# First MLP layer with 512-column and 256-column matmuls per row tile, and a rearranged end chain

## The chip, the cores and the metric

The kernel runs on one core of a Trainium2 chip. The metric is the device time of one execution in microseconds (us); lower is better. The engines are named as in the profile: PE is TensorE's matmul, PEld its weight load, DVE is VectorE, ACT is ScalarE, POOL is GpSimd, and SP is SyncE, whose queue issues most DMAs.

## The reference

One layer of a decoder block over 256 tokens with 2048 channels, all in f32. A normalised input goes through one wide projection, three token mixers (attention, short convolution, a state-space scan) are merged and projected with `w_o`, and then come the parts that matter here:

```python
x = x + (merged @ w_o[i])
h = rms_norm(x, g_mlp[i])
x = x + (jnp.square(jax.nn.relu(h @ w_up[i])) @ w_down[i])     # 2048 -> 8192 -> 2048
gate = jax.nn.sigmoid(rms_norm(x, g_ple[i]) @ w_ple_gate[i])
x = x + ((p[i] @ w_ple[i]) * gate)
return rms_norm(x, g_final)
```

## The kernel before

**Arithmetic.** A product of f32 matrices is made of three matmuls. Each operand is split into a high part (ScalarE rounds it to the fp32r format, `split`, L163 or L166) and a low part (VectorE subtracts the high part from the source, L164 or L167). `mm3` (L171 to L173) issues high*high, high*low and low*high into one PSUM region.

**Weights.** All weights are read once, in pieces of 128 x 1024 f32 (512 KB: two row tiles of 128 by 512 columns), by SP's queue (L75) into six `raw` buffers. `Stream.convert` makes the high part on ScalarE (L87) and the low part on VectorE (L88) into one of four `w` buffers; both are emitted with `high_priority(offset=2000)`. `get(i)` converts one piece ahead of the one that it hands out. A `w` buffer comes free when the matmuls of its piece are done.

**Units.** `unit` computes 512 output columns over a contraction of 2048: four chunks `c`, in each two pieces, in each two row tiles `k`. Kind "A" keeps the tokens stationary and moves 512 weight columns (two token halves `m`, so six matmuls of 512 columns per row tile). Kind "B" keeps four 128-column blocks `s` of the weights stationary and moves the 256 tokens (twelve matmuls of 256 columns per row tile); its output comes out transposed, as the next product wants it. Where "B" is used in the MLP, high and low part of the tokens are two tiles of tag `aT`, eight buffers in all, and the four blocks lie in two PSUM banks.

**PSUM.** There are eight banks: four of tag `acc` for the units, four of tag `s` for transposes and small products.

**The MLP** runs in four quarters `q` of the hidden layer. A quarter has four up units (kind "B", `h2` moving), each followed by `act_job`: ReLU from PSUM on ScalarE (L1130), square on VectorE (L1131), split (L163, L164). Then come four down units (kind "A", `act` stationary), each followed by two VectorE instructions that add the two banks to `x1` (L1150).

**The end.** After the MLP come the gate units, four of kind "A". In the last one the matmuls of token half `m` = 0 come before those of `m` = 1, so that the chain of the first half starts earlier: sigmoid (L1191), multiplication by `pp` in place (L1195), sum with `x1` (L1196), sum of squares (L1198), reciprocal root (`rsqrt`, or L1206 to L1211 with ScalarE's Sqrt for the last one), scaling of four blocks of 512 columns (L1215 to L1221), and the output DMAs on SP's queue (L1223). `dummy` (L1193) is a two-element Sqrt that brings the activation table in early.

**Order.** The Tile framework puts the instructions of each engine in one fixed order, by priority (program order, moved forward by `high_priority`), by its own estimate of when operands are ready, and by when a buffer of the tag is free; each engine then runs its list in that order and waits on semaphores.

Of the kernel before, what the change touches and what calls it, by code (L numbers as in the profile page):

```python
# [15 lines left out]
D = 2048  # L16
T = 256
# [114 lines left out]
def _kern(tc, xT, xn, pT, pos, wbig, consts, colp, rowp, w2p, normg, gfin, cw, out):  # L132
# [24 lines left out]

    def ps(shape=(128, 512)):
        return psum.tile(list(shape), F32, tag="s", name="s", bufs=4)
# [98 lines left out]
    def aT(name):  # L258
        return sb.tile([128, 4, T], R32, tag="aT", name=name, bufs=8)

    hT = []
    for c in range(4):
        h, lo = aT("hTh"), aT("hTl")
# [4 lines left out]
        hT.append((h, lo))  # L268
# [140 lines left out]
    def renorm():  # L409
        for c in range(4):  # L410
            h, lo = aT("hNh"), aT("hNl")
            split(h, lo, xr[c])
            hN.append((h, lo))
# [508 lines left out]
    def unit(kind, lhs, accs, before=None, after=None, apart=False):  # L922

        for c in range(4):
            if before is not None:
                before(c)
            ah, al = lhs[c]
            if apart and c == 3:

                w = [(2, 1, last3)] + [(3, hf, piece()) for hf in range(2)]  # L930
                for m in range(2):
                    for cc, hf, (wh, wl) in w:
                        xh, xl = lhs[cc]
                        for k in range(2):
                            kk = 2 * hf + k
                            mm3(accs[m], (xh[:, kk, sl(m)], xl[:, kk, sl(m)]), (wh[:, k], wl[:, k]),
                                False, cc == 3 and kk == 3)
                break
            for hf in range(2):
                wh, wl = piece()  # L940
                if apart and c == 2 and hf == 1:
                    last3 = (wh, wl)
                    break
                for k in range(2):
                    kk = 2 * hf + k
                    first, last = c == 0 and kk == 0, c == 3 and kk == 3
                    if kind == "A":
                        for m in range(2):
                            mm3(accs[m], (ah[:, kk, sl(m)], al[:, kk, sl(m)]), (wh[:, k], wl[:, k]), first, last)
# [22 lines left out]
    for name, j, _ in units:  # L972
        if name == "small":
            a = acc((128, T))
            n = 0
            for q in range(2):
                wh, wl = piece()
                for k in range(8):
                    xh, xl = hN[n // 4]
                    mm3(a, (wh[:, k], wl[:, k]), (xh[:, n % 4], xl[:, n % 4]), n == 0, n == 15)  # L980
                    n += 1
                side.run(BUDGET)
# [94 lines left out]
    def before_wo(c):  # L1077
        if c == 3:
            side.finish()
        h, lo = aT("mTh"), aT("mTl")  # L1080
        split(h, lo, mg[c])
        mTs[c] = (h, lo)

    def norm_T(n, gains, dst, parts):

        h, lo = aT("h2h"), aT("h2l")
# [6 lines left out]
        dst[n] = (h, lo)  # L1093
# [28 lines left out]
    for q in range(4):  # L1122
        act = {}

        def act_job(a, n, accs):
            h, lo = b4([128, 4, T], R32, name="acth"), b4([128, 4, T], R32, name="actl")
            for i in range(2):
                t = tt([128, 512], name="a")
                with tc.high_priority(offset=1000):
                    S.activation(t, accs[i].rearrange("p s t -> p (s t)"), AF.Relu)  # L1130
                V.tensor_tensor(t, t, t, OP.mult)  # L1131
                split(h[:, sl(i, 2)], lo[:, sl(i, 2)], t.rearrange("p (s t) -> p s t", s=2))
            a[n] = (h, lo)

        for n in range(4):
            accs = [acc((128, 2, 256)) for _ in range(2)]
            if q == 0 and n == 0:
                unit("B", _Drain(h2, side), accs)
# [3 lines left out]
            else:  # L1142
                unit("B", h2, accs)
# [31 lines left out]
    xg, rs4 = {}, {}  # L1175
    for n in range(4):
# [6 lines left out]
        for m in range(2):  # L1183
            final = n == 3 and m == 1
            s4, r = (sm([128, 1], name=q) for q in ("s4", "r4")) if n == 3 else (None, None)
            prio = tc.high_priority(offset=2000) if final else ExitStack()
            with prio:
                parts = [slice(0, 256), slice(256, 512)] if final else [slice(0, 512)]
                s = tt([128, 512], name="sg")
                for q in parts:  # L1190
                    S.activation(s[:, q], accs[m][:, q], AF.Sigmoid, scale=rs3[:, m:m + 1])  # L1191
                if final:
                    S.activation(dummy, s[:, 510:512], AF.Sqrt)  # L1193
                for i, q in enumerate(parts):
                    V.tensor_tensor(s[:, q], s[:, q], pp[n][:, m, q], OP.mult)  # L1195
                    V.tensor_tensor(x1[n][:, m, q], x1[n][:, m, q], s[:, q], OP.add)  # L1196
                    sq = tt([128, 512], name="scr")
                    S.activation(sq[:, q], x1[n][:, m, q], AF.Square, accum_out=ss4[:, m, n + i:n + i + 1])  # L1198
                if not final:
                    G.tensor_tensor(pp[n][:, m], x1[n][:, m], gf[n], OP.mult)  # L1200
                if n < 3:
                    continue
                V.tensor_reduce(s4, ss4[:, m, 0:4 + m], axis=AX.X, op=OP.add)
                if final:
                    v, y, a = sm([128, 1], name="v"), sm([128, 1], name="y"), sm([128, 1], name="a")
                    V.tensor_scalar(v, s4, 1.0 / D, EPS, op0=OP.mult, op1=OP.add)  # L1206
                    S.activation(y, v, AF.Sqrt)
                    V.reciprocal(y, y)
                    V.scalar_tensor_tensor(a, y, -0.5, y, op0=OP.mult, op1=OP.mult)
                    V.tensor_tensor(a, a, v, OP.mult)  # L1210
                    V.scalar_tensor_tensor(r, a, 1.5, y, op0=OP.add, op1=OP.mult)  # L1211
                else:
                    rsqrt(r, s4, 1, D)
            if final:
                V.scalar_tensor_tensor(pp[3][:, m], x1[3][:, m], r, gf[3], op0=OP.mult, op1=OP.mult)  # L1215
                V.tensor_scalar(pp[1][:, m], pp[1][:, m], r, None, op0=OP.mult)
            else:
                for i in (1, 3):
                    G.tensor_tensor(pp[i][:, m], pp[i][:, m], bc(r, [128, 512]), OP.mult)
            S.activation(pp[0][:, m], pp[0][:, m], AF.Copy, scale=r)  # L1220
            S.activation(pp[2][:, m], pp[2][:, m], AF.Copy, scale=r)  # L1221
            for i in (0, 3, 1, 2):
                nc.sync.dma_start(out[:, m, sl(i, 512)], pp[i][:, m])  # L1223
# [98 lines left out]
```

## Time and profile before

| | |
|---|---|
| median of 3 runs | 2020.86 us (2019.52 to 2022.93) |
| the profiled execution | 2019.0 us, span 2017.0 us |
| granted TensorE clock, mean | 0.997 |
| busy share: PE, PEld | 99%, 87% |
| busy share: DVE, ACT, POOL | 66%, 51%, 3% |

Matmuls are pipelined and their recorded durations overlap, so the distance between the starts of two matmuls, and not their duration, is the time that one takes from the engine. Lines are those of the kernel before.

### The profile page before, as it was taken

The numbers are of one execution on the slowest core, as the hardware profiler recorded it, in microseconds if no ns is written. First come the engines' busy times: TensorE is split into PE (matmuls) and PEld (weight loads), VectorE is DVE, ScalarE is ACT, GpSimd is POOL, SyncE is SP. The second block draws the span as 40 slices with busy tenths as digits, with TensorE's granted clock in tenths as the row PEclk, the third lists the DMA queues.
The fourth block names the chain that finished last, engine by engine and source line by source line (L and its number), as shares of the span: only waits on it lengthen the run. The fifth ranks groups of instructions, "written<-read, shape, count | busy, mean of one in ns | idle before, by whom it ended". The sixth has DMA issues, their size and how long they took to land.

```text
span 2017.0 us, 29062 instructions
## 1 busy us (share of the span) xinstructions
PE 1995.5 (99%) x11221; PEld 1747.1 (87%) x11221; DVE 1325.3 (66%) x2095; ACT 1024.3 (51%) x1369; POOL 69.5 (3%) x93
## 2 busy tenths in 40 slices
PE   9999999999999999999999999999999999999997
PEld 7899988898888888898888899889988998998886
DVE  8877768766777668776878665555555555555665
ACT  7556646454655455544645464434433443445554
POOL 1000000000000000000000000000000000000011
PEclk9999999999999999999999999999999999999998
DMA  8556666555665565656675555555555555565552
GB/s 336 188 186 211 194 204 203 194 195 176 211 204 199 174 203 202 206 171 199 208 248 179 184 178 180 190 196 183 183 194 191 180 188 196 186 201 189 187 188 104
DMA packets 110267, 392.91 MB, mean 195 GB/s; under 512 B 12628, under 2 KB 13012, under 8 KB 110128
## 3 DMA queue, kind: packets, MB, share of 16 engines
q1 hardware_dynamic: 103552, 368.71, 54.8%
q0 software_dynamic: 6576, 22.34, 3.6%
q8 instruction: 88, 1.44, 0.3%
q14 instruction: 51, 0.42, 0.1%
HBM read 386.75 MB, written 4.25 MB: 194 GB/s over the span
## 4 chain that ended last, share of the span: by engine, by line
PE 51%; DVE 1%; issue 0%; ACT 0%; DMA 0%; POOLq 0%; POOL 0%; ACTq 0%
PE acc L171 17%; PE acc L173 17%; PE acc L172 17%; PE s L431 1%; DVE w L88 0%; DMA cv<-scrx 0%; PE s L171 0%; PE s L173 0%; PE s L172 0%; PE s L850 0%; ACT L720 0%; ACT scr L1198 0%; POOLq L1315 0%; DVE x L1196 0%; ACT w L87 0%
## 5 line engine op out<-in xcount | busy, mean ns | idle before, releaser
L88 DVE TENSOR_TENSOR w<-raw,w 128x1024 fp32r<-128x1024 f32 x686 | 840.0, 1225 | 587.9 <-ACT w L87 585.7
L87 ACT ACTIVATE w<-raw 128x1024 fp32r<-128x1024 f32 x686 | 726.1, 1059 | 827.8 <-PE acc L173 698.4
L171 PE MATMUL acc<-w,hNh 128*128 128x512 f32 x1024 | 403.9, 394 | 0.0
L173 PE MATMUL acc<-w,hNl 128*128 128x512 f32 x1024 | 399.3, 390 | 0.0
L172 PE MATMUL acc<-w,hNh 128*128 128x512 f32 x1024 | 399.2, 390 | 0.0
L171 PE MATMUL acc<-h2h,w 128*128 128x256 f32 x1024 | 290.0, 283 | 0.0
L173 PE MATMUL acc<-h2h,w 128*128 128x256 f32 x1024 | 289.8, 283 | 0.0
L172 PE MATMUL acc<-h2l,w 128*128 128x256 f32 x1024 | 289.8, 283 | 0.0
L173 PEld LDWEIGHTS acc<-w,hNl 128*128 128x128 f32 x1024 | 192.2, 188 | 41.2
L172 PEld LDWEIGHTS acc<-w,hNh 128*128 128x128 f32 x1024 | 192.5, 188 | 37.2
L171 PEld LDWEIGHTS acc<-w,hNh 128*128 128x128 f32 x1024 | 192.3, 188 | 37.2
L171 PE MATMUL acc<-w,acth 128*128 128x512 f32 x512 | 199.8, 390 | 0.0
L173 PE MATMUL acc<-w,actl 128*128 128x512 f32 x512 | 199.3, 389 | 0.0
L172 PE MATMUL acc<-w,acth 128*128 128x512 f32 x512 | 199.2, 389 | 0.0
L172 PEld LDWEIGHTS acc<-h2l,w 128*128 128x128 f32 x1024 | 196.6, 192 | 0.1
L171 PEld LDWEIGHTS acc<-h2h,w 128*128 128x128 f32 x1024 | 196.6, 192 | 0.1
L173 PEld LDWEIGHTS acc<-h2h,w 128*128 128x128 f32 x1024 | 196.6, 192 | 0.0
L171 PE MATMUL acc<-hNh,w 128*128 128x256 f32 x464 | 132.4, 285 | 0.0
L173 PE MATMUL acc<-hNh,w 128*128 128x256 f32 x464 | 131.3, 283 | 0.0
L172 PE MATMUL acc<-hNl,w 128*128 128x256 f32 x464 | 131.2, 283 | 0.0
L173 PEld LDWEIGHTS acc<-w,actl 128*128 128x128 f32 x512 | 96.1, 188 | 20.1
L172 PEld LDWEIGHTS acc<-w,acth 128*128 128x128 f32 x512 | 96.2, 188 | 19.6
(358 smaller groups left out, 2428.0 us busy)
## 6 DMA issues: line engine op xcount, KB each, us to landing
raw<-wbig SPq DMA_DIRECT2D x686, 512.0 KB, 3.3
cv<-scrx POOLq DMA_DIRECT2D x16, 512.0 KB, 6.1
cw<-cw POOLq DMA_DIRECT2D x8, 512.0 KB, 5.5
E<-acsd POOLq DMA_DIRECT2D x16, 256.0 KB, 4.8
xb<-xn SPq DMA_DIRECT2D x4, 512.0 KB, 10.0
scrx<-ev POOLq DMA_DIRECT2D x4, 512.0 KB, 5.5
x<-xn SPq DMA_DIRECT2D x4, 512.0 KB, 7.1
out<-pp SPq DMA_DIRECT2D x8, 256.0 KB, 2.2
```

What stands on the lines that cost most here:

```text
L87: nc.scalar.activation(w[:, 0], s, AF.Copy)
L88: nc.vector.tensor_tensor(w[:, 1], s, w[:, 0].bitcast(F32), OP.subtract)
L171: PE.matmul(o, ah, bh, start=start, stop=False)
L172: PE.matmul(o, ah, bl, start=False, stop=False)
L173: PE.matmul(o, al, bh, start=False, stop=stop)
L431: PE.transpose(p[:, sl(g)], src[:, sl(g)], ident)
```

## The change

1. The `aT` tiles become [128, 4, 2, T] with high and low part of a row tile side by side (four buffers in place of eight halves); `part` picks one part where a kind "A" unit wants it.
2. A new kind "P" replaces "B" in the MLP's up units. Per row tile it issues four matmuls of 512 columns (weight high part against both parts of the tokens) and then four of 256 (weight low part against the tokens' high part). Each block `s` has a PSUM bank of its own, `[128, 2, T]`; a unit takes four banks, from tag `acc` for even `n` and from tag `s` for odd `n`.
3. `act_job` joins the two halves of each bank first: ScalarE copies the second half to SBUF, VectorE adds the first half to it (`join`). ReLU and square then are one VectorE instruction, max(t,0)*t.
4. In the end chain, the multiplication by `pp` writes a new tile `t`; the second part's sum of squares moves to VectorE; of the first half only block 0 is scaled ahead of the last chain, and its other three blocks wait for `r1`, a copy of `r0` that VectorE makes after the last chain's reciprocal; GpSimd scales nothing more; the seven output DMAs that are left are issued in a new order, one of them on ScalarE's queue.

```diff
+    def halves(tag):
+        return [psum.tile([128, 2, T], F32, tag=tag, name="half", bufs=4) for _ in range(4)]
...
     def aT(name):
-        return sb.tile([128, 4, T], R32, tag="aT", name=name, bufs=8)
+        return sb.tile([128, 4, 2, T], R32, tag="aT", name=name, bufs=4)
+
+    def part(a, i, kk, q):
+        return a[i][:, kk, q] if isinstance(a, tuple) else a[:, kk, i, q]
...
                     else:
                         for s in range(4):
-                            mm3(accs[s // 2][:, s % 2], (wh[:, k, sl(s)], wl[:, k, sl(s)]), (ah[:, kk], al[:, kk]),
-                                first and s % 2 == 0, last and s % 2 == 1)
+                            PE.matmul(accs[s], wh[:, k, sl(s)], a[:, kk], start=first, stop=False)
+                        for s in range(4):
+                            PE.matmul(accs[s][:, 0], wl[:, k, sl(s)], a[:, kk, 0], start=False, stop=last)
...
+    def join(dst, u, a):
+        S.activation(u, a[:, 1], AF.Copy)
+        V.tensor_tensor(dst, a[:, 0], u, OP.add)
...
             for i in range(2):
-                t = tt([128, 512], name="a")
+                t, u = tt([128, 2, T], name="a"), tt([128, 2, T], name="al")
                 with tc.high_priority(offset=1000):
-                    S.activation(t, accs[i].rearrange("p s t -> p (s t)"), AF.Relu)
-                V.tensor_tensor(t, t, t, OP.mult)
-                split(h[:, sl(i, 2)], lo[:, sl(i, 2)], t.rearrange("p (s t) -> p s t", s=2))
+                    for s in range(2):
+                        join(t[:, s], u[:, s], accs[2 * i + s])
+                V.scalar_tensor_tensor(t, t, 0.0, t, op0=OP.max, op1=OP.mult)
+                split(h[:, sl(i, 2)], lo[:, sl(i, 2)], t)
...
         for n in range(4):
-            accs = [acc((128, 2, 256)) for _ in range(2)]
-            if q == 0 and n == 0:
-                unit("B", _Drain(h2, side), accs)
+            accs = halves(("acc", "s")[n % 2])
+            unit("P", _Drain(h2, side) if q == n == 0 else h2, accs)
...
+    def gated(n, m, a, parts):
+        s, t = tt([128, 512], name="sg"), tt([128, 512], name="sp")
+        for q in parts:
+            S.activation(s[:, q], a[:, q], AF.Sigmoid, scale=rs3[:, m:m + 1])
+        if len(parts) > 1:
+            S.activation(dummy, s[:, 510:512], AF.Sqrt)
+        for i, q in enumerate(parts):
+            V.tensor_tensor(t[:, q], s[:, q], pp[n][:, m, q], OP.mult)
+            V.tensor_tensor(x1[n][:, m, q], x1[n][:, m, q], t[:, q], OP.add)
+            sq = tt([128, 512], name="scr")
+            if i == 0:
+                S.activation(sq[:, q], x1[n][:, m, q], AF.Square, accum_out=ss4[:, m, n:n + 1])
+            else:
+                V.tensor_tensor_reduce(sq[:, q], x1[n][:, m, q], x1[n][:, m, q], 1.0, 0.0, OP.mult, OP.add,
+                                       ss4[:, m, n + 1:n + 2])
...
+            if m == 0:
+                V.tensor_reduce(s4, ss4[:, m, 0:4], axis=AX.X, op=OP.add)
+                rsqrt(r, s4, 1, D)
+                S.activation(pp[0][:, m], pp[0][:, m], AF.Copy, scale=r)
+                nc.sync.dma_start(out[:, m, sl(0, 512)], pp[0][:, m])
+                r0 = r
+                continue
...
+                S.activation(y, v, AF.Sqrt)
+                V.reciprocal(y, y)
+
+                V.tensor_copy(r1, r0)
+                V.scalar_tensor_tensor(a, y, -0.5, y, op0=OP.mult, op1=OP.mult)
...
+            for eng, i, q in ((S, 1, 0), (S, 0, 1), (V, 1, 1), (S, 2, 1), (V, 2, 0), (V, 3, 0)):
+                rq = (r1, r)[q]
+                if eng is S:
+                    S.activation(pp[i][:, q], pp[i][:, q], AF.Copy, scale=rq)
                 else:
...
+                    V.tensor_scalar(pp[i][:, q], pp[i][:, q], rq, None, op0=OP.mult)
+            for i, q in ((2, 0), (3, 0), (1, 0), (0, 1), (3, 1), (1, 1), (2, 1)):
+                (S if (i, q) == (2, 1) else nc.sync).dma_start(out[:, q, sl(i, 512)], pp[i][:, q])
```

## Rows read from the trace of the kernel before

**Rows 1.** The page, busy time per engine: us, share of the span, instructions.
```profile
PE 1995.5 (99%) x11221; PEld 1747.1 (87%) x11221; DVE 1325.3 (66%) x2095; ACT 1024.3 (51%) x1369; POOL 69.5 (3%) x93
```
**Rows 2.** Windows by stage: length, busy us and count per engine, PEclk, DMA share, GB/s.
```profile
1207.04:1230.08 23.04, 23.04 (x195) 23.04 (x194) 12.35 (x13) 10.59 (x12) 0.00 (x0) 1.00 0.54 182
1276.16:1363.20 87.04, 87.04 (x390) 72.27 (x389) 45.50 (x43) 36.08 (x36) 0.00 (x0) 1.00 0.58 193
```
**Rows 3.** Timeline of an up unit, PE: start us, duration us, engine, line.
```profile
1225.75 0.28 PE L172 MATMUL acc<-h2l,w 128*128 128x256 f32 x1
...
1234.87 0.28 PE L173 MATMUL acc<-h2h,w 128*128 128x256 f32 x1
```
**Rows 4.** Timeline of a down unit, PE, twelve matmuls apart.
```profile
1300.26 0.39 PE L171 MATMUL acc<-w,acth 128*128 128x512 f32 x1
...
1302.98 0.39 PE L171 MATMUL acc<-w,acth 128*128 128x512 f32 x1
```
**Rows 5.** Timeline where a down unit ends and the next up unit begins.
```profile
1362.75 1.23 DVE L88 TENSOR_TENSOR w<-raw,w 128x1024 fp32r<-128x1024 f32 x1 [1.49 <-ACT w L87]
...
1363.89 1.40 DVE L1150 SCALAR_TENSOR_TENSOR x<-acc,r,x 128x512 f32<-128x512 f32 x2
1363.95 0.39 PE L173 MATMUL acc<-w,actl 128*128 128x512 f32 x1
...
1364.18 0.28 PE L171 MATMUL acc<-h2h,w 128*128 128x256 f32 x1
```
**Rows 6.** Timeline of ACT and DVE around the end of an up unit.
```profile
1228.35 1.06 ACT L87 ACTIVATE w<-raw 128x1024 fp32r<-128x1024 f32 x1 [1.82 <-PE acc L173]
1230.51 0.60 ACT L1130 ACTIVATE a<-acc 128x512 f32<-128x512 f32 x1 [1.10 <-PE acc L173]
...
1232.32 1.23 DVE L88 TENSOR_TENSOR w<-raw,w 128x1024 fp32r<-128x1024 f32 x1 [0.49 <-ACT w L87]
```
**Rows 7.** Timeline of the wo stage: a VectorE sum of 256 columns from PSUM.
```profile
1109.62 0.41 DVE L855 TENSOR_TENSOR y<-y,s 128x256 f32<-128x256 f32 x1
```
**Rows 8.** Timeline of the end.
```profile
2004.20 0.84 ACT L1191 ACTIVATE sg<-acc,rs 128x256 f32<-128x256 f32 x2 [1.18 <-PE acc L173]
...
2005.05 0.42 DVE L1195 TENSOR_TENSOR sg<-sg,pp 128x256 f32<-128x256 f32 x1
2005.06 1.28 ACT L1193 ACT_TABLE_LOAD   x1
2005.39 0.15 DVE L281 TENSOR_TENSOR a<-a,v 128x1 f32<-128x1 f32 x1
2005.51 0.42 DVE L1196 TENSOR_TENSOR x<-x,sg 128x256 f32<-128x256 f32 x1
...
2006.59 0.88 DVE L1195 TENSOR_TENSOR sg<-sg,pp 128x256 f32<-128x256 f32 x1 [0.59 <-ACT dummy L1193]
...
2007.50 1.14 DVE L1196 TENSOR_TENSOR x<-x,sg 128x256 f32<-128x256 f32 x1
2008.72 0.42 ACT L1198 ACTIVATE scr<-x 128x256 f32<-128x256 f32 x1 [1.16 <-POOL pp L1219]
...
2009.27 0.16 DVE L1203 TENSOR_REDUCE s<-ss 128x1 f32<-128x5 f32 x1 [0.62 <-ACT scr L1198]
...
2010.56 0.16 DVE L1211 SCALAR_TENSOR_TENSOR r<-a,y 128x1 f32<-128x1 f32 x1
2010.75 0.72 ACT L1220 ACTIVATE pp<-pp,r 128x512 f32<-128x512 f32 x1 [0.81 <-DVE r L1211]
2010.75 0.75 DVE L1215 SCALAR_TENSOR_TENSOR pp<-x,r,gf 128x512 f32<-128x512 f32 x1
...
2011.42 0.48 DVE L1216 TENSOR_SCALAR pp<-pp,r 128x512 f32<-128x512 f32 x1
```
**Rows 9.** Windows of the last output transfers: columns as in rows 2.
```profile
2012.00:2012.50 0.50, 0.00 (x0) 0.00 (x0) 0.00 (x0) 0.08 (x1) 0.00 (x0) 0.50 0.29 115
...
2015.00:2015.50 0.50, 0.00 (x0) 0.00 (x0) 0.00 (x0) 0.00 (x0) 0.00 (x0) 0.50 0.23 82
```

More of the change, by code (lines that the diff above doesn't have):

```diff
@@ L410, in renorm @@
         for c in range(4):
-            h, lo = aT("hNh"), aT("hNl")
-            split(h, lo, xr[c])
-            hN.append((h, lo))
+            a = aT("hN")
+            split(a[:, :, 0], a[:, :, 1], xr[c])
+            hN.append(a)
     def rope(dst, src, m):
@@ L932, in unit @@
                     for cc, hf, (wh, wl) in w:
-                        xh, xl = lhs[cc]
                         for k in range(2):
                             kk = 2 * hf + k
-                            mm3(accs[m], (xh[:, kk, sl(m)], xl[:, kk, sl(m)]), (wh[:, k], wl[:, k]),
+                            mm3(accs[m], [part(lhs[cc], i, kk, sl(m)) for i in range(2)], (wh[:, k], wl[:, k]),
                                 False, cc == 3 and kk == 3)
@@ L948, in unit @@
                         for m in range(2):
-                            mm3(accs[m], (ah[:, kk, sl(m)], al[:, kk, sl(m)]), (wh[:, k], wl[:, k]), first, last)
+                            mm3(accs[m], [part(a, i, kk, sl(m)) for i in range(2)], (wh[:, k], wl[:, k]), first, last)
+                    elif kind == "B":
+                        for s in range(4):
+                            mm3(accs[s // 2][:, s % 2], (wh[:, k, sl(s)], wl[:, k, sl(s)]), (a[:, kk, 0], a[:, kk, 1]),
+                                first and s % 2 == 0, last and s % 2 == 1)
                     else:
                         for s in range(4):
-                            mm3(accs[s // 2][:, s % 2], (wh[:, k, sl(s)], wl[:, k, sl(s)]), (ah[:, kk], al[:, kk]),
-                                first and s % 2 == 0, last and s % 2 == 1)
+                            PE.matmul(accs[s], wh[:, k, sl(s)], a[:, kk], start=first, stop=False)
+                        for s in range(4):
+                            PE.matmul(accs[s][:, 0], wl[:, k, sl(s)], a[:, kk, 0], start=False, stop=last)
                 side.run(BUDGET)
@@ L978, in _kern @@
                 for k in range(8):
-                    xh, xl = hN[n // 4]
-                    mm3(a, (wh[:, k], wl[:, k]), (xh[:, n % 4], xl[:, n % 4]), n == 0, n == 15)
+                    x = [part(hN[n // 4], i, n % 4, slice(0, T)) for i in range(2)]
+                    mm3(a, (wh[:, k], wl[:, k]), x, n == 0, n == 15)
                     n += 1
@@ L1079, in before_wo @@
             side.finish()
[L1080 to L1082 removed]
+        mTs[c] = aT("mT")
+        split(mTs[c][:, :, 0], mTs[c][:, :, 1], mg[c])
     def norm_T(n, gains, dst, parts):
[L1086 removed]
+        a = aT("h2")
+        h, lo = a[:, :, 0], a[:, :, 1]
         for m in range(2):
@@ L1183, in _kern @@
         for m in range(2):
[L1184 to L1211, printed above, removed]
-                else:
-                    rsqrt(r, s4, 1, D)
@@ L1214, in _kern @@
[L1214 to L1223, printed above, removed]
+            if n < 3 or m == 0:
+                gated(n, m, accs[m], [slice(0, 512)])
+                G.tensor_tensor(pp[n][:, m], x1[n][:, m], gf[n], OP.mult)
```

25 lines of the change are left out of this document (18 added, 7 removed).

## The prediction

> **What bounds the kernel now.** I read the page first: PE is busy for 1995.5 us, 99% of the span, the next engine, VectorE, for 1325.3 [rows 1]. Busy PE alone proves nothing, because recorded matmuls overlap, so I went to the windows by stage and from there to the distance between starts. An up unit lasts 23.04 us with PE busy for all of it at granted clock 1.00 (the 2.4 GHz level), while VectorE works 12.35 us, ScalarE 10.59 us, and the DMAs are busy by half [rows 2]. In the timeline of such a unit two matmuls of 256 columns that are 76 places apart start 9.12 us apart: 120.0 ns each [rows 3]. One up unit has 4 chunks x 4 row tiles x 4 blocks x 3 = 192 of them, and 192 x 120.0 ns = 23.04 us, exactly the unit. So there PE issues without a pause, and nothing else sets the time. In a down unit twelve matmuls of 512 columns take 2.72 us: 226.7 ns each [rows 4]. The step from 256 to 512 columns costs 106.7 ns, which is 256 columns at 2.4 GHz; taken off 120.0 it leaves 13.3 ns, and twice taken off 226.7 it leaves 13.3 ns again. A matmul in this kernel costs its columns plus 13.3 ns, whatever its width.
>
> **The up units: what two matmuls in place of three are worth.** Per row tile and block the old form pays three times 120.0 = 360.0 ns. The new form moves the same 768 columns in one matmul of 512 and one of 256: 226.7 + 120.0 = 346.7 ns. The saving is one fixed cost, 13.3 ns. There are 4 quarters x 4 units x 16 row tiles x 4 blocks = 1024 such triples: 1024 x 13.3 ns = **13.65 us**. PEld too is busy for the whole up unit [rows 2], but whether load or matmul sets the 120.0 ns doesn't matter: the new 256-column matmuls come four in a row, each with its load, as in rows 3, and the 512-column ones with theirs as in rows 4. Where the widths meet, the trace already has the change: the last 512-column matmul of a down unit starts at 1363.95, the next (256) at 1364.18, 0.23 us later [rows 5], no more than usual. That every matmul now goes to another PSUM bank than the one ahead of it should cost nothing: the old form changes bank after six matmuls, and the 120.0 ns of rows 3 contain these changes.
>
> The Trainium skill ("TensorE: Matmul & The Clock Gate", section Back-to-back issue gap) speaks against this size: it puts the warm isolated gap at columns / 2.4 + 2.5 ns, a fixed part of 2.5 ns. By it the same 1024 matmuls would be worth 1024 x 2.5 ns = 2.6 us (an estimate from that page). The trace does not agree: 13.3 ns at both widths [rows 3, 4].
>
> **PSUM banks.** A unit now takes four banks, not two. Between up units this costs nothing: even and odd units use different tags, so a bank is wanted again only a whole unit (about 22 us) after it was left, against a few us of evacuation. At the entry of a quarter it differs: the down unit before has just left its two banks, and the old up unit started on the other two. VectorE empties them with two sums from 1363.89 to 1365.29; the up unit's first matmul starts at 1364.18 [rows 5]. In the new order block 3 wants its bank three 512-column matmuls later, at 1364.86, and gets it at 1365.29: 0.43 us late. Were VectorE caught by another weight conversion of 1.23 us ahead of the sums [rows 5], it would be 1.7 us. Four entries (the first comes after the wo stage, which ends in the same way) give 4 x 0.43 = 1.7 us if PE keeps the written order, and 0 if the planner, which knows that a bank is not free, puts the second row tile's matmuls of blocks 0 and 1 ahead. I take between the two, where the planner hides a bit more than half: **+0.7 us**, ends 0 and 4 x 1.7 = 6.8.
>
> **Evacuation.** Per up unit the two ReLUs of 0.60 us [rows 6] become four copies of 256 columns (the nearest row is the sigmoid pair, 0.84 us for two [rows 8]), so ScalarE goes from 10.59 to about 11.1 us. VectorE gains four sums of 256 columns at 0.41 us [rows 7], and its two squares become max-and-multiply, at most 0.75 us each like the fused instruction of rows 8: below 12.35 + 1.64 + 1.50 = 15.5 us even if the old squares are not taken off. The unit itself shrinks to 64 x 346.7 ns = 22.19 us, so both stay far under it. What hides this work is the supply of weights: a piece of eight such pairs of matmuls lasts 2.77 us, there are four `w` buffers, and ScalarE is seen waiting 1.82 us for PE to free one [rows 6]. A conversion that begins when a piece ends has three pieces, 8.3 us, until it is wanted and needs 1.06 + 1.23 = 2.3 us: 6.0 us of cover. If four copies and four sums (3.3 us in all) stood ahead of it, it would still be in time. DMA: 512 KB per 2.77 us, about 189 GB/s, is less than the 193 GB/s of the down units [rows 2]. Cost: nothing.
>
> **Tile tags.** High and low part are now freed together. They were last read one matmul apart, 0.23 us at most, and the splits that reuse them run a unit or more ahead. Nothing.
>
> **The end.** Here the chain is worth reading instruction by instruction [rows 8]. The second multiplication waits for `dummy` until 2006.59, since it overwrites what `dummy` reads, and it and the sum behind it take 0.88 and 1.14 us, where the first part's take 0.42 each; GpSimd, for which the square at 2008.72 is shown waiting, scales in that stretch. The new tile `t` takes the wait away and an idle GpSimd, as I read it, the slowness: first sum done at 2005.93, then two times 0.42 and the sum of squares on VectorE. No row shows that instruction; 0.42 (a 256-column product) and 0.75 (a fused 512-column one) bound it, and I take the middle. The second part is done at about 2007.35, the first part's square on ScalarE a little before (behind the table load that ends at 2006.34). The reduction starts at about 2007.45 in place of 2009.27: 1.8 us earlier.
>
> What is late next: the copy `r1` adds 0.2 us to the chain, so `r` comes at 2010.72 - 1.8 + 0.2 = 2009.1, and `r1` three small steps of 0.2 us ahead of it, at 2008.5. Two scalings of the first half (0.48 us each) may slip in between these steps, as L281 of the other half's root does now between L1195 and L1196. But the end is set by the output transfers. Before, four blocks followed `r`. The windows show a share of 0.29 in the half microsecond from 2012.0 and 0.23 in that from 2015.0: data flowed from 2012.35 to 2015.1 [rows 9], 0.69 us per block, and began 0.9 us after the first scaling's end at 2011.47 [rows 8]. Now seven blocks remain, 4.8 us. If the two scalings slip in, block (2, 0) is ready at 2009.0, data flow from 2009.9 to 2014.7: 0.4 us earlier. If they queue behind the last chain, (2, 0), which heads SP's queue, is ready only at about 2009.1 + 0.75 + 2 x 0.48 = 2010.8, and data end at 2016.5: 1.4 us later. Since gaps are filled so in rows 8, I take **-0.4 us**, ends -0.8 (the sum of squares at its lower bound and a shorter start of the transfers) and +1.4.
>
> **The sum.** -13.65 + 0.7 - 0.4 = -13.35 us. The profiled execution took 2019.0 us, 2.0 of them outside its span, so it would take 2005.65. The median of the runs lies 1.86 us above that execution: 2020.86 - 13.35 = **2007.5 us**, 0.66% faster.
>
> **Rivals.**
> *Bank waits in full.* Every entry of a quarter waits for the two sums with a weight conversion ahead, 1.7 us each, 6.8 in all, and the end gives 1.4 back: 2020.86 - 13.65 + 6.8 + 1.4 = 2015.4. For it: VectorE's conversion of 1362.75 stands right ahead of the sums [rows 5]. Against: it ends 0.09 us behind the first sum's start, so it delayed little. Chance 0.08.
> *The fixed cost is paid per 256 columns when a matmul follows another bank.* Then the 512-column one costs 240 ns and nothing is saved: 2020.86 + 0.7 - 0.4 = 2021.2, no change. For it: the down units' 226.7 ns come from three matmuls in a row into one bank. Against: no bank change in rows 3 shows. Chance 0.05. The gap rule of the Trainium skill ("TensorE: Matmul & The Clock Gate") would land in the same class, at 2018.6 with the other terms kept.
> *Evacuation blocks the weights: slower.* If ScalarE's and VectorE's lists put the next conversion behind the whole job of a unit, copies, sums, and twice square and split (1.7 + 1.6 + 2 x 3 x 0.75 = 7.8 us), that is 1.8 us more than the cover of 6.0 us, and PE waits 1.8 us in each of 16 units: 28.8 us, 2007.5 + 28.8 = 2036.3. It decides from 13.35 / 16 = 0.83 us per unit on. Against: conversions are moved forward by 2000 places and the job's first part by 1000, and now a conversion is done among the job's instructions [rows 6]. Chance 0.04.
>
> **Numbers.** The forecast has 0.83, with 2004.5 to 2010 as its own range: its faster end is the end chain at -0.8 with no bank wait (2006.4) less the 2 us by which runs of one kernel differ. The whole range goes to 2012, half of the way to the full bank waits, and down to 2003.8; some 0.17 is left out. A measurement of this kernel tells about 0.2%, 4 us, from no change. Faster: the forecast and the bank rival, 0.91. Same: 0.05. Slower: 0.04.
>
> **What would show it.** Up units of 22.2 us with starts 226.7 and 120.0 ns apart bear out the main term; 240 ns after a bank change refutes it. PE waiting at the first matmuls of a quarter, released by L1150's sums, is the bank wait. L1195's second part without a wait and near 0.42 us, and the reduction some 3.3 us after the last sigmoids' start, bear out the end; a DMA share near 1.0 from block (2, 0) on shows that transfers set the last microseconds. The prediction is wrong if PE waits for `w` in the up units, or if the 512-column matmuls take longer than those of the down units.

## The result, and the profile after

The changed kernel takes 2009.7 us (median of 4 runs, 2008.96 to 2010.98) against 2020.3 us in the runs beside it: ratio 0.995, 95% interval 0.9937 to 0.9962, or about 10 us less. 13.35 us less had been forecast: 2007.5 us for the median, within 2003.8 to 2012.0. The interval leaves no doubt that the kernel got faster; a difference of half a per cent is small all the same, so most of what follows is read from stretches of the profiles.

The page of the changed kernel, busy time per engine (answers to [rows 1]):

```profile
PE 1988.0 (99%) x10197; PEld 1693.5 (84%) x10197; DVE 1346.4 (67%) x2164; ACT 1024.9 (51%) x1399; POOL 67.5 (3%) x91
```

PE has 1024 matmuls fewer and is still busy all the time, which by itself says nothing; the spacing of starts does. Its windows, columns as in [rows 2], first a stretch of one unit's length within the up units of the second quarter, then the down units of the first quarter:

```profile
1420.65:1443.05 22.40, 22.40 (x130) 19.57 (x129) 13.63 (x16) 10.61 (x14) 0.00 (x0) 1.00 0.56 188
1276.50:1363.50 87.00, 87.00 (x387) 72.11 (x386) 46.81 (x47) 36.09 (x38) 0.00 (x0) 1.00 0.59 192
```

Timeline of the same up unit, PE; "x4" is four matmuls in a row, the first number the start of the first of them:

```profile
1420.30 0.63 PE L968 MATMUL half<-h,w 128*128 128x256 f32 x4
1420.77 1.09 PE L966 MATMUL half<-h,w 128*128 128x512 f32 x4
1421.69 0.64 PE L968 MATMUL half<-h,w 128*128 128x256 f32 x4
1422.17 1.09 PE L966 MATMUL half<-h,w 128*128 128x512 f32 x4
```

One row tile goes from 1420.77 to 1422.17: 1.40 us for four pairs, 350 ns a pair. The forecast had 346.7. The wide ones (512 columns) take 0.92 us for four, the narrow ones (256) 0.48. Over the 28 row tiles between 1400 and 1440 the single starts of the same trace give 232.2 ns for a wide one, in place of 226.7, and 118.6 for a narrow one, in place of 120.0.

The length of a unit can be read off VectorE, since a weight conversion starts when PE frees a buffer, and the conversions of one unit are eight. Timeline of VectorE, two conversions eight apart in the second quarter:

```profile
1411.20 1.22 DVE L88 TENSOR_TENSOR w<-raw,w 128x1024 fp32r<-128x1024 f32 x1
...
1433.66 1.22 DVE L88 TENSOR_TENSOR w<-raw,w 128x1024 fp32r<-128x1024 f32 x1
```

That is 22.46 us, as in the third and fourth quarter; in the first it is 22.40. Before it was 23.04.

The whole stretch from the first up matmul to the sigmoids of the last half (timeline of PE and of ACT):

```profile
1186.85 0.95 PE L966 MATMUL half<-h,w 128*128 128x512 f32 x3
...
1997.98 0.84 ACT L1199 ACTIVATE sg<-acc,rs 128x256 f32<-128x256 f32 x2 [1.13 <-PE acc L177]
```

811.13 us in place of 820.17 (1184.03 to 2004.20): **9.04 us less**. From the sigmoids to the end of the span it is 11.22 us (1997.98 to 2009.2) in place of 12.80: **1.58 us less**. The two add up to 10.6 us. Ahead of the MLP this execution lost 2.8 us (1186.85 against 1184.03). That stretch differs from one execution to the next (end_only below shows that it is not the change): in the other kernels' profiles, whose code there is that of the changed kernel, the MLP began between 1185.05 and 1188.72. Of the four runs the profiled one took longest, 2010.98 us, while the profiled execution of the kernel before was faster than every other run of it on record.

The end, timeline (answers to [rows 8]):

```profile
1998.88 0.42 DVE L1203 TENSOR_TENSOR sp<-sg,pp 128x256 f32<-128x256 f32 x1
...
1999.28 0.42 DVE L1203 TENSOR_TENSOR sp<-sg,pp 128x256 f32<-128x256 f32 x1
1999.62 0.75 DVE L1204 TENSOR_TENSOR x<-x,sp 128x256 f32<-128x256 f32 x2
...
2000.40 0.42 DVE L1209 CUSTOM_DVE_ANT_0 scr<-x 128x256 f32<-128x256 f32 x1
...
2000.94 0.16 DVE L1236 TENSOR_REDUCE s<-ss 128x1 f32<-128x5 f32 x1
...
2001.32 0.20 ACT L1239 ACTIVATE y<-v 128x1 f32<-128x1 f32 x1
2001.37 0.15 DVE L1242 COPY r<-r 128x1 f32<-128x1 f32 x1
...
2001.62 0.49 DVE L1253 TENSOR_SCALAR pp<-pp,r 128x512 f32<-128x512 f32 x1
2002.03 0.16 DVE L1240 RECIPROCAL y<-y 128x1 f32<-128x1 f32 x1
2002.10 0.47 DVE L1253 TENSOR_SCALAR pp<-pp,r 128x512 f32<-128x512 f32 x1
...
2002.86 0.16 DVE L1245 SCALAR_TENSOR_TENSOR r<-a,y 128x1 f32<-128x1 f32 x1
```

The second multiplication no longer waits and takes 0.42 us, and the sum of squares on VectorE takes 0.42 as well. The two scalings of the first half stand inside the last chain, the first of them ahead of the reciprocal, in the time in which VectorE would wait for ScalarE's root. Windows of the output transfers (answers to [rows 9]):

```profile
2002.00:2002.50 0.50, 0.00 (x0) 0.00 (x0) 0.50 (x4) 0.28 (x1) 0.00 (x0) 0.50 0.56 221
...
2007.00:2007.50 0.50, 0.00 (x0) 0.00 (x0) 0.00 (x0) 0.00 (x0) 0.00 (x0) 0.50 1.02 385
2007.50:2008.00 0.50, 0.00 (x0) 0.00 (x0) 0.00 (x0) 0.00 (x0) 0.00 (x0) 0.50 0.65 254
```

All eight blocks flow from 2002.2 to 2007.8 with almost no pause. Counted from the last sigmoids they end at 9.85 us, before at about 10.9; both are estimates from the share of the last well-filled window.

### The profile page after: what moved, and what is told of

Its sections match the earlier page's. It is cut to its first block, busy times and chain, and to the rows that moved or that the text cites. A ratio compares the mean times of both kernels' runs of the same rounds, so it can differ in the third digit from the quotient of the medians.

```text
span 2009.2 us, 27111 instructions
## 1 busy us (share of the span) xinstructions
PE 1988.0 (99%) x10197; PEld 1693.5 (84%) x10197; DVE 1346.4 (67%) x2164; ACT 1024.9 (51%) x1399; POOL 67.5 (3%) x91
## 4 chain that ended last, share of the span: by engine, by line
PE 51%; DVE 1%; issue 0%; ACT 0%; DMA 0%; ACTq 0%; DVEq 0%; POOLq 0%
PE half L966 12%; PE acc L177 11%; PE acc L175 11%; PE acc L176 11%; PE half L968 6%; PE s L441 1%; DVE w L88 0%; DMA cv<-scrx 0%; PE s L175 0%; PE s L177 0%; PE s L176 0%; PE s L860 0%; DVE sp L1203 0%; DVE x L1204 0%; ACT pp L1251 0%
## 5 line engine op out<-in xcount | busy, mean ns | idle before, releaser
L175 PE MATMUL acc<-w,hN 128*128 128x512 f32 x1024 | 404.3, 395 | 0.0
L177 PE MATMUL acc<-w,hN 128*128 128x512 f32 x1024 | 399.7, 390 | 0.0
L176 PE MATMUL acc<-w,hN 128*128 128x512 f32 x1024 | 399.6, 390 | 0.0
L966 PE MATMUL half<-h,w 128*128 128x512 f32 x1024 | 280.3, 395 | 0.0
L177 PEld LDWEIGHTS acc<-w,hN 128*128 128x128 f32 x1024 | 192.5, 188 | 41.2
L175 PEld LDWEIGHTS acc<-w,hN 128*128 128x128 f32 x1024 | 192.8, 188 | 37.3
L176 PEld LDWEIGHTS acc<-w,hN 128*128 128x128 f32 x1024 | 192.8, 188 | 37.3
L966 PEld LDWEIGHTS half<-h,w 128*128 128x128 f32 x1024 | 175.0, 189 | 24.0 <-DVE x L1170 1.0
L968 PEld LDWEIGHTS half<-h,w 128*128 128x128 f32 x1024 | 157.2, 189 | 22.1
L968 PE MATMUL half<-h,w 128*128 128x256 f32 x1024 | 163.5, 281 | 0.0
L175 PE MATMUL acc<-hN,w 128*128 128x256 f32 x464 | 132.5, 285 | 0.0
L177 PE MATMUL acc<-hN,w 128*128 128x256 f32 x464 | 131.3, 283 | 0.0
L176 PE MATMUL acc<-hN,w 128*128 128x256 f32 x464 | 131.2, 283 | 0.0
L176 PEld LDWEIGHTS acc<-w,acth 128*128 128x128 f32 x512 | 96.1, 188 | 19.9
L175 PEld LDWEIGHTS acc<-w,acth 128*128 128x128 f32 x512 | 96.1, 188 | 19.8
L176 PEld LDWEIGHTS acc<-hN,w 128*128 128x128 f32 x464 | 89.0, 192 | 0.2
```

Of the source, the lines that this page charges most:

```text
L175: PE.matmul(o, ah, bh, start=start, stop=False)
L176: PE.matmul(o, ah, bl, start=False, stop=False)
L177: PE.matmul(o, al, bh, start=False, stop=stop)
L966: PE.matmul(accs[s], wh[:, k, sl(s)], a[:, kk], start=first, stop=False)
L968: PE.matmul(accs[s][:, 0], wl[:, k, sl(s)], a[:, kk, 0], start=False, stop=last)
```

## The experiments

The layer's 9.04 us are 4.6 less than the 13.65 of the forecast. Where did they go? The table gives, from each profile, the length of an up unit (eight weight conversions apart; quarters that differ are listed), the stretch from the first up matmul to the last half's sigmoids, and from there to the end of the span. The ideal of 346.7 ns a pair is 22.19 us a unit. Each ratio is to the runs of the kernel before that were made beside it, whose medians were 2020.3 to 2021.95 us.

| kernel | up unit, us | MLP to sigmoids, us | end, us | median of runs, us | ratio to before (95%) |
|---|---|---|---|---|---|
| before | 23.04 | 820.17 | 12.80 | 2020.3 | |
| changed | 22.40, 22.46 | 811.13 | 11.22 | 2009.7 | 0.995 (0.9937 to 0.9962) |
| layer_only | 22.40, 22.46 | 811.10 | 12.26 | 2011.18 | 0.9949 (0.9936 to 0.9961) |
| end_only | 23.04 | 820.18 | 11.20 | 2019.33 | 0.9988 (0.9979 to 0.9997) |
| order_block | 22.62, 22.18, 22.61, 22.61 | 811.66 | 11.45 | 2011.19 | 0.9946 (0.993 to 0.9963) |
| order_block_again | 22.62, 22.19, 22.19, 22.19 | 808.36 | 11.50 | 2008.39 (one run) | |
| order_two | 22.29 | 808.32 | 11.51 | 2007.73 (one run) | |
| order_piece | 22.35 | 809.65 | 11.45 | 2008.95 | 0.994 (0.9926 to 0.9955) |
| order_pair | 22.35 | 809.12 | 11.35 | 2009.3 | 0.994 (0.9925 to 0.9955) |
| order_chunk | 22.27 | 808.42 | 11.47 | 2008.69 | 0.9936 (0.9921 to 0.995) |
| down_s | 22.40, 22.46 | 810.62 | 11.42 | 2010.81 | 0.9942 (0.9928 to 0.9956) |
| end_r0 | 22.40, 22.46 | 811.11 | 11.24 | 2009.79 | 0.9939 (0.9926 to 0.9953) |
| snake | 22.23 | 807.16 | 11.24 | 2007.23 | 0.9927 (0.9914 to 0.9941) |

The up unit and the MLP stretch repeat to some hundredths of a us where nothing was changed in them (811.13, 811.10, 811.11), so tenths count there. The column for the end is good to some 0.05 us, since spans are printed to 0.1. The medians are good to a us or two.

**layer_only and end_only: the two parts alone.** The first has the new units and evacuation and the end of before, the second the reverse (joint tiles in both).

> The new first layer with the old end. If the layer brings 9.1 us (by the times of the weight conversions in the two profiles, from -2.8 to +6.2 us) and the end 1.6 us, this is 9.1 us faster than the kernel before and the span from the last half's sigmoids to the end stays at 12.8 us. Rival: the two influence each other (the planner lays out the end differently), then the parts don't add up to the 10.6 us of the whole.

> The old first layer (192 matmuls of 256 columns per unit, joint tiles of high and low part) with the new end. From the last half's sigmoids to the end 11.2 us in place of 12.8, so 1.6 us faster than the kernel before. If the 2.8 us that the profile of the changed kernel lost ahead of the MLP come from the joint tiles, they show here too, as a loss between 730 and 800 us, and the kernel is about 1 us slower than before; if they are chance, they don't.

The parts add up in the stretches: 9.07 us from the layer, 1.6 from the end, neither touching the other's. By the medians' ratios the layer is worth 10.3 us (7.9 to 12.9) and the end 2.4 (0.6 to 4.2). One thing did not come as expected: with the old end the span's last stretch was 12.26 and not 12.80 us, though its instructions stand as before. The windows say where. First layer_only, then the kernel before:

```profile
2009.50:2010.00 0.50, 0.00 (x0) 0.00 (x0) 0.00 (x0) 0.00 (x0) 0.00 (x0) 0.50 0.68 250
2010.00:2010.50 0.50, 0.00 (x0) 0.00 (x0) 0.00 (x0) 0.00 (x0) 0.00 (x0) 0.50 0.00 0
```

```profile
2015.50:2016.00 0.50, 0.00 (x0) 0.00 (x0) 0.00 (x0) 0.00 (x0) 0.00 (x0) 0.50 0.02 8
```

The bulk of layer_only's transfers ends 10.9 us behind its sigmoids (1998.94), as in the kernel before. But in the kernel before a few packets came late: the records of single packets have the last one land 11.47 us behind the sigmoids, in layer_only 11.02, in the changed kernel 9.97. From that last packet to the end of the span all three took nearly the same, 1.33, 1.24 and 1.25 us. So of the 1.58 us at the end, 1.05 belong to the change and some 0.5 to late packets in the one profile of before.

The loss of 2.8 us ahead of the MLP is not the joint tiles' price. The profiles alone would not show that: all twelve profiles with joint tiles have the MLP begin later (1185.05 in end_r0 to 1188.72 in end_only) than the one profile without them (1184.03). The runs do. Take from the span of each run the two stretches that repeat, 820.18 + 12.80 us for the kernel before and 820.18 + 11.24 for end_only, and 1184.4 to 1188.9 us are left ahead of the MLP in the 15 runs of before, and 1184.4 to 1188.7 in the 11 of end_only beside them: the same range, with and without joint tiles.

**order_block: narrow right behind wide.**

```diff
                         for s in range(4):
                             PE.matmul(accs[s], wh[:, k, sl(s)], a[:, kk], start=first, stop=False)
-                        for s in range(4):
                             PE.matmul(accs[s][:, 0], wl[:, k, sl(s)], a[:, kk, 0], start=False, stop=last)
```

> The up units of the changed kernel take 22.40 us (1.400 us per row tile), where 226.7 and 120.0 ns per matmul would give 22.19. Here the 256-column matmul of a block follows right behind its 512-column one, so PE goes back from 256 to 512 columns 64 times per unit in place of 16. Theory S (each return from 256 to 512 columns costs another 13.3 ns): 22.19 + 64 x 0.0133 = 23.04 us per unit, the whole gain of the layer gone, some 10 us slower than the changed kernel. Theory B (a 512-column matmul costs about 5.8 ns more when it goes to another PSUM bank than its predecessor) and theory R (the first nine or so 512-column matmuls behind any 256-column ones run at 231 ns, as at the start of a down unit): 22.4 us, no change.

None of the three held. The units do not take 23.04 us, so a fixed price of 13.3 ns for every return from 256 to 512 columns is refuted. They do not take 22.4 either: three quarters ran at 22.61 and one at 22.18, the ideal. Timeline of PE: the first two rows are of the first quarter, eight pairs apart, the last two of the second, twelve pairs apart:

```profile
1229.67 0.40 PE L966 MATMUL half<-h,w 128*128 128x512 f32 x1
...
1232.50 0.40 PE L966 MATMUL half<-h,w 128*128 128x512 f32 x1
...
1404.73 0.39 PE L966 MATMUL half<-h,w 128*128 128x512 f32 x1
...
1408.89 0.39 PE L966 MATMUL half<-h,w 128*128 128x512 f32 x1
```

2.83 us for eight pairs is 353.8 ns, 4.16 us for twelve is 346.7 ns. Same order of matmuls, same tags of banks and tiles, granted clock 1.00 in both.

**order_block_again: the same kernel once more.**

> The block order once more, unchanged. In its first profile the up units of one quarter took 22.18 us (346.7 ns per pair of matmuls) and those of the other three 22.61 (353.5 ns), with the same matmul order. If the step is fixed by the program, the second quarter is the quick one again; if it is chance (a state that PE's pipeline falls into at the entry of a quarter and keeps), other quarters are quick, or none.

This time quarters 2 to 4 were at 22.19, only the first at 22.62. VectorE's conversions, eight apart, in the second quarter:

```profile
1410.92 1.23 DVE L88 TENSOR_TENSOR w<-raw,w 128x1024 fp32r<-128x1024 f32 x1
...
1433.11 1.22 DVE L88 TENSOR_TENSOR w<-raw,w 128x1024 fp32r<-128x1024 f32 x1
```

22.19 us. So where widths alternate PE runs in one of two states, taken up at the entry of a quarter and kept through its four units: 346.7 or 353.6 ns a pair. The third and fourth quarter went either way in two executions of one program, so it is not the program alone that picks. The two executions were on different chips, and the first quarter was slow and the second quick in both; chance and chip are not separated by any run.

**order_two, order_piece, order_pair, order_chunk: longer runs.** With runs of two, eight, eight with each bank twice in a row, and sixteen:

```diff
-                        for s in range(4):
-                            PE.matmul(accs[s], wh[:, k, sl(s)], a[:, kk], start=first, stop=False)
-                        for s in range(4):
-                            PE.matmul(accs[s][:, 0], wl[:, k, sl(s)], a[:, kk, 0], start=False, stop=last)
+                    for k, s in [(k, s) for k in range(2) for s in range(4)]:
+                        PE.matmul(accs[s], wh[:, k, sl(s)], a[:, 2 * hf + k], start=c + hf + k == 0, stop=False)
+                    for k, s in [(k, s) for k in range(2) for s in range(4)]:
+                        PE.matmul(accs[s][:, 0], wl[:, k, sl(s)], a[:, 2 * hf + k, 0], start=False,
+                                  stop=c == 3 and hf + k == 2)
```

That is order_piece. order_pair turns the loops around (`for s in range(4) for k in range(2)`), order_chunk takes both pieces of a chunk and loops over its four row tiles, and order_two keeps the row tile and does blocks 0 and 1, then 2 and 3:

```diff
-                        for s in range(4):
-                            PE.matmul(accs[s], wh[:, k, sl(s)], a[:, kk], start=first, stop=False)
-                        for s in range(4):
-                            PE.matmul(accs[s][:, 0], wl[:, k, sl(s)], a[:, kk, 0], start=False, stop=last)
+                        for h2_ in range(2):
+                            for s in (2 * h2_, 2 * h2_ + 1):
+                                PE.matmul(accs[s], wh[:, k, sl(s)], a[:, kk], start=first, stop=False)
+                            for s in (2 * h2_, 2 * h2_ + 1):
+                                PE.matmul(accs[s][:, 0], wl[:, k, sl(s)], a[:, kk, 0], start=False, stop=last)
```

> Per weight piece eight matmuls of 512 columns and then eight of 256: 8 returns per unit in place of 16. Theory S: 22.19 + 8 x 0.0133 = 22.29 us per up unit, 1.7 us in all less than the changed kernel. Theory B (bank change): every 512-column matmul still changes bank, 22.4 us. Theory R (first nine slow): all eight are among the first nine, 22.4 us.

> As eight and eight per piece, but block by block: two 512-column matmuls in a row into the same bank. Theory B: only every second one changes bank, half of the excess of 0.21 us is left, 22.29 us per up unit. Theory S: 8 returns, 22.29 us as without the pairing, so pairing itself adds nothing. Theory R: 22.4 us.

> Per chunk (two pieces) sixteen matmuls of 512 columns and then sixteen of 256: 4 returns per unit. Theory S: 22.19 + 4 x 0.0133 = 22.24 us per up unit, 2.5 us in all less than the changed kernel. Theory R: nine of sixteen slow, 22.31 us. Theory B: 22.4 us. A w buffer is held longer here; if that starves PE, it shows as waits for VectorE's w.

> Runs of two: two matmuls of 512 columns, two of 256, so 32 returns from narrow to wide per unit. Measured so far, per return and by the length of the wide run: 1: 6.6 ns (or 0 in one quarter), 4: 13 to 16 ns, 8 and 16: 20 ns. Theory L (a return costs some 4 to 6 ns on each of the first wide matmuls, up to 20 ns in all): about 10 ns per return, 22.5 us per up unit. Rival (only two states exist, with or without a fixed loss per unit): 22.2 or 22.6 us.

Pairing banks adds nothing to a unit (22.35 with and without), so theory B is refuted: a change of bank between matmuls is free here, as the prediction had it. (The stretch of order_pair is 0.53 us shorter than order_piece's for another reason, told under down_s.) Longer runs help: the excess over 22.19 is 0.16 us a unit with runs of eight, 0.08 with sixteen, against 0.21 to 0.27 with four. Per return that is 20 ns with eight and with sixteen, 13 to 17 with four. Theory R (nine slow wide ones) says 0.12 for sixteen where 0.08 was measured, and 0.21 for eight where 0.16 was; its direction held and its size did not.

Where the excess sits can be read from single starts. In order_pair's timeline the second row is the same view begun at the sixth wide matmul of the run of eight:

```profile
1403.96 2.00 PE L956 MATMUL half<-h,w 128*128 128x512 f32 x8
1405.12 0.84 PE L956 MATMUL half<-h,w 128*128 128x512 f32 x3
1405.80 1.11 PE L958 MATMUL half<-h,w 128*128 128x256 f32 x8
1406.75 2.00 PE L956 MATMUL half<-h,w 128*128 128x512 f32 x8
```

The first five wide ones behind narrow ones take 1.16 us, 232 ns each, and the other three 0.68, 226.7 each. The single starts of this trace say 233, 236, 228, 232 and 231 ns for the first five, 27 ns above the steady price together; behind them the first two narrow ones take 113 and 119 ns and give 8 back. That is the 20 ns per return of the long runs, the same in order_piece, order_chunk and snake, and a run of four ends before it has paid in full. So theory R had the place right, with five matmuls and not nine.

The kernel before does the same where narrow matmuls are followed by wide ones, at the end of its first quarter's up units (timeline of PE):

```profile
1277.11 0.40 PE L171 MATMUL acc<-w,acth 128*128 128x512 f32 x1
...
1278.27 0.39 PE L173 MATMUL acc<-w,actl 128*128 128x512 f32 x1
...
1279.41 0.39 PE L172 MATMUL acc<-w,acth 128*128 128x512 f32 x1
```

Five wide matmuls in 1.16 us, 232 ns each, and the next five in 1.14, 227 each.

Theory L's size failed at runs of two: timeline of VectorE of order_two, eight conversions apart, and of order_chunk likewise:

```profile
1409.43 1.23 DVE L88 TENSOR_TENSOR w<-raw,w 128x1024 fp32r<-128x1024 f32 x1
...
1431.72 1.22 DVE L88 TENSOR_TENSOR w<-raw,w 128x1024 fp32r<-128x1024 f32 x1
```

```profile
1411.14 1.21 DVE L88 TENSOR_TENSOR w<-raw,w 128x1024 fp32r<-128x1024 f32 x1
...
1433.41 1.21 DVE L88 TENSOR_TENSOR w<-raw,w 128x1024 fp32r<-128x1024 f32 x1
```

22.29 us in all four quarters of order_two (one execution), 0.10 over the ideal where 0.3 was expected: 3 ns per return. Its two wide ones cost 13 ns more than the steady price and its two narrow ones 10 ns less. Runs of four, the change's own, are dearer than runs of two, eight or sixteen.

**down_s: free banks at the entry of a quarter.**

```diff
-            accs = [acc(), acc()]
+            accs = [ps(), ps()] if n == 3 and q < 3 else [acc(), acc()]
             unit("A", act, accs)
```

> The last down unit of quarters 0 to 2 takes its two banks from tag s, so that the next quarter's first up unit finds four free banks of tag acc. Theory (bank wait at the entry): the three waits of PE's weight loads for the sums of the down unit (1.0 us in all) and the detour of the matmul order vanish, a quarter lasts 0.3 to 0.4 us less, 1.0 to 1.2 us in all. Rival: the entry loses because the width changes there, whatever the banks: no change.

In the changed kernel the waits of the weight loads say so (view of who waited for whom; total us, times, longest), and the timeline shows the order turned around at the entry, three wide, three narrow, then the fourth block:

```profile
PEld half L966 <- DVE x L1170: 1.0, 3, 0.3
```

```profile
1364.19 1.40 DVE L1170 SCALAR_TENSOR_TENSOR x<-acc,r,x 128x512 f32<-128x512 f32 x2
1364.25 0.39 PE L177 MATMUL acc<-w,actl 128*128 128x512 f32 x1
...
1364.48 1.01 PE L966 MATMUL half<-h,w 128*128 128x512 f32 x3
...
1365.33 0.52 PE L968 MATMUL half<-h,w 128*128 128x256 f32 x3
1365.69 0.64 PE L966 MATMUL half<-h,w 128*128 128x512 f32 x2
```

The same place in down_s:

```profile
1364.46 0.39 PE L177 MATMUL s<-w,actl 128*128 128x512 f32 x1
1364.69 1.07 PE L966 MATMUL half<-h,w 128*128 128x512 f32 x4
1365.60 0.64 PE L968 MATMUL half<-h,w 128*128 128x256 f32 x4
```

The waits are gone and the order is straight, and the stretch is 0.51 us shorter (810.62), 0.17 per entry: the mechanism as expected, at half the size. The expectation took the load's wait for the matmul's. The trace of the changed kernel shows the difference: the load waited 0.32 us, and the first three wide matmuls of the entry took 0.85 us (1364.48 to 1365.33) in place of 0.68, 0.17 lost. The pair order_piece and order_pair shows the same price a second time: order_piece has the same three waits (1.0 us), order_pair, which comes to the fourth bank later, has none, and its quarters 2 to 4 are 0.18 us shorter each. The median of the runs can't show half a us.

**end_r0: no copy, the first half's blocks as early as they fit.**

```diff
-                V.tensor_copy(r1, r0)
...
-                rq = (r1, r)[q]
+                rq = (r0, r)[q]
```

> No copy r1: the first half's blocks are scaled with r0 as soon as the planner finds a gap, so they may slip into the last chain earlier. Theory T (the end is set by eight output transfers at 380 GB/s, which run without a pause from the first scaled block on): the last chain's r comes up to 1 us later, but the transfers begin up to 1 us earlier and the end with them: 0.5 to 1 us less from the sigmoids to the end than 11.2. Theory C (the last chain's r sets the end): 0.5 to 1 us more.

Its output windows:

```profile
1999.50:2000.00 0.50, 0.00 (x0) 0.00 (x0) 0.50 (x4) 0.50 (x2) 0.00 (x0) 0.50 0.07 16
2000.00:2000.50 0.50, 0.00 (x0) 0.00 (x0) 0.20 (x3) 0.34 (x2) 0.00 (x0) 0.50 0.75 287
...
2005.50:2006.00 0.50, 0.00 (x0) 0.00 (x0) 0.00 (x0) 0.00 (x0) 0.00 (x0) 0.50 0.35 131
2006.00:2006.50 0.50, 0.00 (x0) 0.00 (x0) 0.00 (x0) 0.00 (x0) 0.00 (x0) 0.50 0.01 4
```

Its sigmoids start at 1996.16. The transfers begin 3.8 us behind them in place of 4.2, and the bulk ends 9.5 us behind in place of 9.85; the root `r` comes at the same distance (5.06 us, and 5.04 in the changed kernel). That is theory T's mechanism, 0.35 us of it where 0.5 to 1 was expected, and against theory C, which expected a later end. But the span did not shrink (11.24 us): here a few packets came late, as the last row shows, and the last one landed 9.98 us behind the sigmoids, in the changed kernel 9.97. It can't be settled at this size, and copy or none makes no measured difference.

**snake: what helped, together.** Sixteen wide and sixteen narrow per chunk, every second chunk in the opposite order, with the edits of down_s and end_r0.

```diff
+                    for wide in ((1, 0) if c % 2 == 0 else (0, 1)):
+                        for kk, s in ks:
+                            w_ = both_hf[kk // 2][1 - wide][:, kk % 2, sl(s)]
+                            o_, a_ = (accs[s], a[:, kk]) if wide else (accs[s][:, 0], a[:, kk, 0])
+                            PE.matmul(o_, w_, a_, start=wide == 1 and c + kk == 0, stop=wide == 1 and c + kk == 6)
```

> All that helped in one kernel: per chunk sixteen wide and sixteen narrow matmuls, every second chunk in the opposite order (two returns per unit), the last down unit of quarters 0 to 2 on the banks of tag s, and the end without the copy r1. By theory L (20 ns per return of a long run): 22.19 + 2 x 0.02 = 22.23 us per up unit; entries free. Against the changed kernel 16 x 0.21 = 3.4 us from the units and 0.5 us from the entries: 3.9 us less. If the returns are not what costs, units stay at 22.27 us or more.

Units of 22.23 us as worked out, and the stretch is 807.16 us, 3.97 less than the changed kernel's, as expected; 0.64 is left to the 806.52 of 346.7 ns a pair. 2007.23 us at the median, ratio 0.9927 (0.9914 to 0.9941). It is the fastest version found; the difference to the changed kernel rests on the stretches of the profiles, as the intervals of the two ratios still overlap.

## Why the prediction was right, and where its sizes were off

- **What bounds the kernel.** Right: PE's spacing of starts sets the time of the MLP, and taking a matmul out of each triple shortened it. VectorE rose to 13.63 us per unit and no conversion came late.
- **13.65 us from the up units.** Right in mechanism, too large: 4 units at 0.64 and 12 at 0.58 us make 9.5 us. The step that was off is the one that said of the new 512-column matmuls that they cost "as in rows 4". They did not: a pair cost 350.0 to 350.9 ns, so a matmul taken out was worth 9 to 10 ns and not 13.3. [rows 3, 4] are each a steady stream of one width, and the sum took the two prices over into a mixture. The prediction had named this as a sign of being wrong ("if the 512-column matmuls take longer than those of the down units"), and it came: 232.2 ns against 226.7. The time stayed in the range because the excess was 4.1 us of 13.65. The border that the prediction looked at [rows 5] goes from wide to narrow, where nothing is lost. The trace of the kernel before has the other direction too, from 1277.11 on, and there the first five wide matmuls already took 232 ns each. Before the change that border came once a quarter in the MLP; the change puts it into every row tile. The rival that the fixed cost is paid twice when the bank changes is refuted by order_pair; its time of no change was not approached.
- **The Trainium skill's gap rule** ("TensorE: Matmul & The Clock Gate", section Back-to-back issue gap; a fixed part of 2.5 ns for an isolated matmul) would have given 2.6 us for the layer, an estimate from that page. The layer alone brought 9.07 us in its stretch. The trace decides: in this stream the part of a matmul that doesn't scale with its columns is worth several times that.
- **+0.7 us for the banks at the entries.** Right in kind and near in size: 9.5 less the 9.04 measured leaves 0.5, and down_s got 0.51 back. The planner did turn the order around, though not as supposed: it put three narrow matmuls of the same row tile ahead of the fourth block, not the second row tile's. Bank waits in full, the rival, did not come.
- **Evacuation and tile tags at nothing.** Right: no wait of PE for `w` appears between 1183 and 1905, and the loss ahead of the MLP is not the tiles' (end_only).
- **-0.4 us at the end.** Right in mechanism (transfers set it, they ran without a pause), too small: 1.05 us by the bulk of the transfers. The prediction had block (2, 0) ready 4.8 us behind the sigmoids; it was ready at 2002.1 (the end of the first L1253), 4.1 behind, because the planner put the copy and this scaling ahead of the reciprocal, into VectorE's wait for ScalarE.
- **The sum.** 4.1 too much at the units, 0.2 too much loss at the entries, 0.65 to 1.2 too little at the end: -13.35 forecast, -10.1 to -10.6 by the parts, -10.6 by the medians. The entries and the end made up for a part of what was missing at the units.

Left open: why a mixture of widths is dearer. It is not the bank. Where the excess sits is shown, in the first five wide matmuls behind narrow ones, but no run shows what slows these. Between 3 and 20 ns per return were measured, by the length of the runs, and with alternating widths two states, 0 and 7 ns.

## What to carry to other kernels

Where PE is the bound, count matmuls as well as columns: one instruction of 512 columns in place of two of 256 was worth 9 to 13 ns each time, 9 us here over 1024. Prices of two steady streams do not add up exactly in a mixture; look at a border of the two in both directions, measure a unit of the mixture, and try the order of widths, for runs of two or sixteen were cheaper than runs of four, and no other cost showed in their profiles. At a kernel's end look at when the first output block leaves, not only at when the last is computed.

## What the runs showed of the hardware that was not expected

- One instruction order on PE, with the granted clock at 1.00, ran at 346.7 ns a pair of matmuls in some stretches and at 353.6 in others, decided at the entry of a stretch of four units and kept for 90 us. Two executions of one program, on two chips, differed by 3.3 us through this alone (811.66 and 808.36).
- The first five wide matmuls behind narrow ones cost 232 ns on average in place of 226.7, in the kernel before (from 1277.11) as in order_pair (from 1403.96); runs of four were dearer than runs of two, eight or sixteen.
- With GpSimd idle, VectorE's product and sum of 256 columns in the end took 0.42 us each; while GpSimd scaled they took 0.88 and 1.14, in the kernel before and again in layer_only (0.88 and 1.15).
- The last packets of the output can land late: in two executions of the same end code the bulk ended 10.9 us behind the last sigmoids, the last packet at 11.47 in one (before) and 11.02 in the other (layer_only), and the span ended 1.2 to 1.3 us behind that packet.
